# Expert layers: order of the searches and look-ups, look-up table in pairs

## The chip, the cores and the metric

The kernel runs on one core of one Trainium2 chip. The metric is the device time in microseconds; three runs give a median. One execution more is recorded by the hardware profiler, and all rows below come from it.

## The reference, cut to what matters

Two networks run one after the other over 256 tokens of width 1024: a two-layer block (attention and SwiGLU) and then a second two-layer block, whose feed-forward part is an expert lookup. The change touches only that part, which runs twice, once for each layer of the second block:

```python
def peer_ffn(h, w_q, sub_keys, u_tab, v_tab):
    q = (h @ w_q).reshape(B, S, PEER_HEADS, 2, PEER_DQ // 2)
    scores = jnp.einsum('bshpd,hpkd->bshpk', q, sub_keys)
    s1, i1 = lax.top_k(scores[..., 0, :], 16)
    s2, i2 = lax.top_k(scores[..., 1, :], 16)
    cand_s = (s1[..., :, None] + s2[..., None, :])      # 16 x 16 candidates
    cand_id = (i1[..., :, None] * 128 + i2[..., None, :])
    top_s, top_pos = lax.top_k(cand_s, 16)
    ids = jnp.take_along_axis(cand_id, top_pos, axis=-1)
    gate = jax.nn.softmax(top_s, axis=-1)
    ...
    act = jax.nn.gelu(jnp.einsum('thkd,td->thk', u_tab[idx], hx))
    return jnp.einsum('thk,thkd->td', g * act, v_tab[idx])
```

There are 8 heads and 128 x 128 = 16384 experts, each with a row of 1024 in `u_tab` and in `v_tab`.

## The kernel before

`peer(l)` doesn't gather rows. It multiplies all tokens with all experts, 128 tiles of 128 experts each, and sets to zero what wasn't chosen. `M` holds [128, 128 tiles, 256 tokens]: the GELU of each product times its gate.

- *Scores and first level.* 16 products with `wq` give the queries, `score` multiplies them with the keys, and `first_level` finds the 16 best of 128 for each of 16 half heads and both token halves `a` on VectorE (lines 1629 to 1633; maximum, index, replacement, maximum, index: 32 such searches).
- *Expert tiles.* The loop over `NEXP` = 128 calls `u_tile(i)`: a weight tile `raw` of 128 x 1024 is loaded from `pu` by SP's queue; ScalarE rounds it to `hi` (L258); `lo` = `raw` - `hi` is made on VectorE or GpSimd (L259), as `lo_pat` says, "V" or "P"; TensorE then runs 16 products with `hi` and 8 with `lo` (L320), the `hi` ones first. `raw`, `hi` and `lo` have three buffers each. ScalarE applies GELU (L1771).
- *The side list.* `todo` holds the expert choice and the gates as entries (cost, function), some with "P". After each `u_tile` the loop looks at the first entry: with "P" the next tile's `lo` goes to GpSimd and the budget grows by 2.4, else it goes to VectorE and the budget grows by 1.7. Entries are issued as long as the budget covers the first one's cost.
- *The entries.* `second_level(h, a)`: 16 x 16 sums (L1667) and the same five search steps (L1671 to L1675), 8 heads for each token half. `begin(a)`: subtracts the maximum (L1691), copies the first-level indices to a BF16 table `IB` (L1692) and splits the found positions into row and column (`HS`). `look_up(s, a)`: compares with all 16 numbers (L1701), multiplies with the table (L1702), and adds up in halves (L1704, L1705). `exponents`: one exponential on ScalarE for both halves (L1708). `weights`: sum, reciprocal, product. `turn(a)`: three transposes on TensorE (L1725) and copies. `gates(g)`: 64 entries, for four tokens each, which build one-hot operands on VectorE (L1746, L1750), multiply them on TensorE (L1756), and apply the gate to the tiles of `M` already made on VectorE (L1761) or leave it for tiles to come by ScalarE (L1763).
- *Order.* Each engine works through its queue in order. The queue isn't the source's order: a planner at compile time, with its own estimate of durations, places each instruction when its operands are ready, the source's order deciding among ready ones. What it places early and what isn't ready on the chip holds up all behind it.

After the loop `accumulate_tokens` multiplies `M` with the 128 tiles of `pv` (L1442 to L1444).

Of the kernel before, what the change touches and what calls it, by code (L numbers as in the profile page):

```python
# [13 lines left out]
U32 = mybir.dt.uint32  # L14
AF = mybir.ActivationFunctionType
ALU = mybir.AluOpType
# [155 lines left out]
class Kernel:  # L172
# [1310 lines left out]
    def lru(self, l):  # L1483
        nc, tc, A = self.nc, self.tc, self.A
        with self.stream(3, 3), tc.tile_pool(name="lru", bufs=1) as pool:
# [7 lines left out]
            IG = pool.tile([128, 2, KT, T], F32, name="IG")  # L1493
            HS = pool.tile([128, 2, KT, T], F32, name="HS")
            self.begin_mod(pool, l, 0, [A["lruin"][n] for n in range(8)], Y, norm=False, squares=HS[:, 0])

            late = pool.tile([128, 3], F32, name="late")

            def zero_after(i, x):
                nc.scalar.activation(late[:, i:i + 1], x, AF.Relu, scale=-1.0)  # L1500
# [20 lines left out]
            for b in range(4):  # L1521
# [4 lines left out]
                for d in range(2):  # L1526
                    hi, lo = self.wsplit(A["lrug"][b, d], (2, 2, 2, 128))
                    for gt in range(2):
# [7 lines left out]
                        for n in range(2):  # L1536
# [6 lines left out]
                            if gt == 0:  # L1543
                                nc.scalar.activation(HS[:, d, k], R[:, d, k], AF.Tanh, scale=w[:, 4, c:c + 1])
                    k2 = slice(2 * b, 2 * b + 2)
# [22 lines left out]
            for i in range(4):  # L1568
                for d in range(2):
                    x = HS[:, d, 2 * i:2 * i + 2]  # L1570
                    nc.scalar.activation(x, x, AF.Sqrt, bias=late[:, 1:2])
            zero_after(2, HS[:, 1, KT - 1, 0:1])

            def recurrence(i):
                ks = slice(2 * i, 2 * i + 2)
                for d in range(2):
                    nc.vector.tensor_tensor(IG[:, d, ks], IG[:, d, ks], HS[:, d, ks], op=ALU.mult)
                    rv = (lambda x: x[:, ::-1]) if d else (lambda x: x)
# [23 lines left out]
    def peer(self, l):  # L1602
        nc, tc, A = self.nc, self.tc, self.A
        with ExitStack() as st:
# [6 lines left out]
            SI = [tail[:, 512 + a * 256:768 + a * 256].rearrange("p (h j) -> p h j", j=16) for a in range(2)]  # L1611
# [4 lines left out]
            IDX = scratch[:, 3072:3840].rearrange("p (i t) -> p i t", t=T)  # L1616
            HB = scratch[:, 3840:4096].rearrange("p (s h j) -> p s h j", h=8, j=16)
# [33 lines left out]
            for hp in range(16):  # L1651
                p, b = self.product(A["wq"][l, hp], gpool,
                                    (IDX[:, 0, 2 * hp:2 * hp + 2], EQ[:, 1024 + hp % 4 * 256:1280 + hp % 4 * 256]))
# [4 lines left out]
            score(15)  # L1658

            todo = deque()  # L1660
            TOP = [IDX[:, 0, a * 128:a * 128 + 128].rearrange("p (h j) -> p h j", j=16) for a in range(2)]
            POS = [IDX[:, 1, a * 128:a * 128 + 128].rearrange("p (h j) -> p h j", j=16) for a in range(2)]

            def second_level(h, a):
                ca, cb = CA[h % 2], CB[h % 2]
                s1, s2 = SV[a][:, 2 * h], SV[a][:, 2 * h + 1]
                nc.vector.tensor_tensor(ca.rearrange("p (a b) -> p a b", b=16),  # L1667
                                        s1[:, :, None].to_broadcast([128, 16, 16]),
                                        s2[:, None, :].to_broadcast([128, 16, 16]), op=ALU.add)
                t, ix = TOP[a][:, h], POS[a][:, h].bitcast(U32)  # L1670
                nc.vector.max(t[:, 0:8], ca)  # L1671
                nc.vector.max_index(ix[:, 0:8], t[:, 0:8], ca)
                nc.vector.match_replace(cb, t[:, 0:8], ca, -3e38)
                nc.vector.max(t[:, 8:16], cb)
                nc.vector.max_index(ix[:, 8:16], t[:, 8:16], cb)  # L1675
# [2 lines left out]

            spare = scratch[:, 4096:4608].bitcast(BF16)
            KK = spare[:, 0:256].rearrange("p (k j) -> p k j", j=16)  # L1680
            HS = spare[:, 256:512].rearrange("p (s h j) -> p s h j", h=8, j=16)
            IB = spare[:, 512:768].rearrange("p (h s j) -> p s h j", s=2, j=16)
            both = EQ.bitcast(BF16)
            EB = both[:, 0:2048].rearrange("p (h k j) -> p h k j", k=16, j=16)
            ws = IDX[:, 2].rearrange("p (h j) -> p h j", j=16)

            def begin(a):
                if a == 0:
                    nc.vector.tensor_copy(KK, self.iota[:, 0:16, None].to_broadcast([128, 16, 16]))
                pos = POS[a].bitcast(U32)  # L1690
                nc.vector.tensor_tensor(ws[:, 8 * a:8 * a + 8], TOP[a], TOP[a][:, :, 0:1].to_broadcast([128, 8, 16]),  # L1691
                                        op=ALU.subtract)  # L1692
                nc.vector.tensor_copy(IB, SI[a].bitcast(U32).rearrange("p (h s) j -> p s h j", s=2))
                nc.vector.tensor_scalar(HB[:, 0].bitcast(U32), pos, 4, None, op0=ALU.logical_shift_right)
                nc.vector.tensor_scalar(HB[:, 1].bitcast(U32), pos, 15, None, op0=ALU.bitwise_and)
                nc.vector.tensor_copy(HS, HB.bitcast(U32))

            def look_up(s, a):
                tt = nc.vector.tensor_tensor
                all_ = [128, 8, 16, 16]  # L1700
                tt(EB, HS[:, s, :, None, :].to_broadcast(all_), KK[:, None].to_broadcast(all_), op=ALU.is_equal)  # L1701
                tt(EB, EB, IB[:, s, :, :, None].to_broadcast(all_), op=ALU.mult)  # L1702
                for n in (8, 4, 2):
                    tt(EB[:, :, :n], EB[:, :, :n], EB[:, :, n:2 * n], op=ALU.add)  # L1704
                tt((TOP[a], POS[a])[s], EB[:, :, 0], EB[:, :, 1], op=ALU.add)  # L1705

            def exponents():
                nc.scalar.activation(ws, ws, AF.Exp)  # L1708

            def weights():  # L1710
                st_ = gpool.tile([128, 2, 16], F32, name="gst", tag="gst", bufs=1)
# [10 lines left out]
            def turn(a):  # L1722
                p = self.ps("ax")
                for i in range(3):
                    nc.tensor.transpose(p[:, i * 128:i * 128 + 128], IDX[:, i, a * 128:a * 128 + 128], self.ident)  # L1725
                ts = slice(a * 128, a * 128 + 128)
                nc.scalar.activation(CT[:, :, ts], p[:, :256].rearrange("p (a b) -> p a b", b=128), AF.Copy)
                w, rest = p[:, 256:384], scratch[:, :128]
                for i in range(3):
                    nc.vector.tensor_copy(W3[:, i, ts], w)  # L1730
                    if i < 2:
                        nc.vector.tensor_tensor(rest, w, W3[:, i, ts], op=ALU.subtract)
                        w = rest
# [44 lines left out]
            def v_operands(i):  # L1778
# [4 lines left out]
                if i == 8:  # L1783
# [5 lines left out]

            second = [[(2.4, lambda h=h, a=a: second_level(h, a), "P") for h in range(8)] for a in range(2)]  # L1790
            turns = [(1.0, lambda a=a: turn(a)) for a in range(2)]
            gate = [(2.2, lambda g=g: gates(g)) for g in range(ng)]
            decode = [[(1.6, lambda a=a: begin(a))] + [(4.8, lambda s=s, a=a: look_up(s, a)) for s in range(2)]
                      for a in range(2)]

            decode[1][2:2] = [(0.0, exponents)]
            todo.extend(second[0] + decode[0] + second[1] + decode[1] + [(0.9, weights), (2.4, lambda: None)])
            todo.extend(turns + gate)
            budget = 0.0
            for i in range(NEXP):  # L1800
# [138 lines left out]
```

## Time and profile before

| | us |
|---|---|
| median of 3 runs | 3066.19 (3064.2 to 3067.69) |
| the profiled execution | 3063.65 |
| its span, first to last instruction | 3061.8 |
| TensorE products busy | 2979.8 (97%) |
| VectorE busy | 2377.9 (78%) |
| ScalarE busy | 1694.7 (55%) |
| GpSimd busy | 176.1 (6%) |
| mean granted TensorE clock | 0.989 |

The profile calls TensorE PE, its weight loads PEld, VectorE DVE, ScalarE ACT and GpSimd POOL. A share over the whole span is a mean over some twenty stages with different limits. What the change is worth has to be read from the stretches in which its instructions lie: about 1287 to 1430 us for layer 0 and 2234 to 2380 us for layer 1 up to the first gates. An idle time in brackets behind a row is that of its engine just before the row, with what ended it.

### The profile page before, as it was taken

To read this page: it belongs to the slowest core of one execution; us is meant where nothing else is said; L and a number is where in the kernel's file an instruction comes from. 1 tells how busy PE (TensorE), PEld (TensorE's weight loads), DVE (VectorE), ACT (ScalarE), POOL (GpSimd) and SP (SyncE) were. 2 spreads that over 40 slices of the span, in tenths; PEclk is the share of its full clock that TensorE was granted. 3 is DMA by queue.
4 is the path that set the end of the run, shared out by engine and by line. 5 is a ranking of instruction groups with operands and counts; after the bars stand their busy time and mean duration, and the time that the engine had idled before them with its cause. 6 is when DMAs were issued, how large, how long until landed. Compare 5 with 4: busy or idle time off the path is not lost.

```text
span 3061.8 us, 53557 instructions
## 1 busy us (share of the span) xinstructions
PE 2979.8 (97%) x20336; PEld 2705.8 (88%) x20336; DVE 2377.9 (78%) x4869; ACT 1694.7 (55%) x3072; POOL 176.1 (6%) x90
## 2 busy tenths in 40 slices
PE   9999999999999999999999999999898999999998
PEld 8888889888688889999999988888898999988887
DVE  8877997986689698798889655557999888855555
ACT  7556755665565467544554555556744555455554
POOL 0000000000100000351000000000062000000000
PEclk9999999999999999999999999999999999999999
DMA  8853785984059533444444555555444444455554
GB/s 308 277 170 97 241 297 180 313 277 156 24 173 311 164 123 125 143 155 158 155 156 153 172 193 193 193 195 183 149 142 156 161 154 157 158 187 193 194 194 140
DMA packets 155346, 556.57 MB, mean 182 GB/s; under 512 B 17360, under 2 KB 19152, under 8 KB 154832
## 3 DMA queue, kind: packets, MB, share of 16 engines
q1 hardware_dynamic: 154800, 552.62, 54.0%
q8 instruction: 160, 2.62, 0.3%
q14 instruction: 98, 0.80, 0.1%
q10 hardware_dynamic: 288, 0.52, 0.1%
HBM read 552.02 MB, written 1.05 MB: 181 GB/s over the span
## 4 chain that ended last, share of the span: by engine, by line
PE 84%; DVE 11%; ACT 3%; issue 1%; DMA 1%; SPq 0%; DVEq 0%; ACTq 0%
PE ps_mm L320 25%; PE ps_mm L339 14%; PE ps_ax L1442 8%; PE ps_ax L1443 8%; PE ps_ax L1444 8%; PE ps_mm L342 7%; PE ps_mm L1756 3%; PE ps_ax L320 2%; PE ps_mm L671 1%; DVE lo L259 1%; PE ps_ax L1279 1%; DVE M L1667 1%; DMA raw<-in_gu_dram 1%; ACT hi L258 1%; DVE M L1631 1%
## 5 line engine op out<-in xcount | busy, mean ns | idle before, releaser
L258 ACT ACTIVATE hi<-raw 128x1024 fp32r<-128x1024 f32 (+1 forms) x952 | 996.1, 1049 | 963.5 <-PE ps_ax L1443 332.6
L259 DVE TENSOR_TENSOR lo<-raw,hi 128x1024 fp32r<-128x1024 f32 (+1 forms) x898 | 1082.8, 1208 | 532.9 <-ACT hi L258 521.7
L320 PE MATMUL ps_mm<-XX,hi 128*128 128x256 f32 (+1 forms) x5664 | 782.9, 288 | 32.4 <-ACT hi L258 20.5
L320 PEld LDWEIGHTS ps_mm<-XX,hi 128*128 128x128 f32 x5664 | 717.4, 191 | 40.3 <-ACT hi L258 21.1
L320 PE MATMUL ps_mm<-XX,lo 128*128 128x256 f32 (+1 forms) x2832 | 408.1, 284 | 9.5 <-DVE lo L259 9.5
L1444 PE MATMUL ps_ax<-lo,ah 128*128 128x512 f32 x1024 | 398.4, 389 | 0.0
L1443 PE MATMUL ps_ax<-hi,al 128*128 128x512 f32 x1024 | 398.4, 389 | 0.0
L1442 PE MATMUL ps_ax<-hi,ah 128*128 128x512 f32 x1024 | 398.3, 389 | 0.0
L320 PEld LDWEIGHTS ps_mm<-XX,lo 128*128 128x128 f32 x2832 | 368.9, 191 | 11.7 <-DVE lo L259 11.5
L339 PE MATMUL ps_mm<-XX,hi 128*128 128x512 f32 x1216 | 308.7, 395 | 2.8 <-ACT sg L501 2.2
L339 PEld LDWEIGHTS ps_mm<-XX,hi 128*128 128x128 f32 x1216 | 218.2, 189 | 44.1 <-ACT sg L501 3.2
L1444 PEld LDWEIGHTS ps_ax<-lo,ah 128*128 128x128 f32 x1024 | 192.3, 188 | 40.1
L1442 PEld LDWEIGHTS ps_ax<-hi,ah 128*128 128x128 f32 x1024 | 192.3, 188 | 39.8
L1443 PEld LDWEIGHTS ps_ax<-hi,al 128*128 128x128 f32 x1024 | 192.3, 188 | 39.6
L259 POOL TENSOR_TENSOR lo<-raw,hi 128x1024 fp32r<-128x1024 f32 x58 | 147.7, 2555 | 1367.7 <-ACT hi L258 1328.7
L342 PEld LDWEIGHTS ps_mm<-XX,lo 128*128 128x128 f32 x1216 | 163.6, 188 | 17.4 <-DVE lo L259 5.0
L339 PE MATMUL ps_mm<-AHL,hi 128*128 128x512 f32 x704 | 177.7, 392 | 0.0
L342 PE MATMUL ps_mm<-XX,lo 128*128 128x256 f32 x1216 | 169.1, 281 | 1.8 <-DVE lo L259 1.7
L1763 ACT ACTIVATE M<-ps_mm 128x376 f32<-128x376 f32 (+42 forms) x128 | 44.7, 349 | 182.8 <-DVE M L1761 182.8
L339 PEld LDWEIGHTS ps_mm<-AHL,hi 128*128 128x128 f32 x704 | 125.6, 188 | 21.9
L1750 DVE TENSOR_TENSOR oh<-first,W 128x768 bf16<-128x768 bf16 x256 | 130.8, 550 | 0.0
L990 DVE SCALAR_TENSOR_TENSOR raw<-raw,one,cb 128x1024 f32<-128x1024 f32 x96 | 122.9, 1281 | 1.5
(455 smaller groups left out, 3754.0 us busy)
## 6 DMA issues: line engine op xcount, KB each, us to landing
raw<-in_pu_dram SPq DMA_DIRECT2D x256, 512.0 KB, 3.2
raw<-in_pv_dram SPq DMA_DIRECT2D x256, 512.0 KB, 3.2
raw<-in_gu_dram SPq DMA_DIRECT2D x175, 512.0 KB, 4.8
raw<-in_ada_dram SPq DMA_DIRECT2D x96, 512.0 KB, 4.5
raw<-in_down_dram SPq DMA_DIRECT2D x64, 512.0 KB, 4.6
raw<-in_hgin_dram SPq DMA_DIRECT2D x32, 512.0 KB, 3.3
raw<-in_wq_dram SPq DMA_DIRECT2D x32, 512.0 KB, 3.2
raw<-in_down_dram SPq DMA_DIRECT2D x32, 384.0 KB, 3.9
```

The lines of the kernel that those rows point to most:

```text
L258: self.nc.scalar.activation(hi, src, AF.Copy)
L259: (eng or self.lo_engine()).tensor_tensor(lo, src, hi, op=ALU.subtract)
L320: mm(out, w[a][:, k], xin[b][:, k0 + k], start=k0 == 0 and at == 0, stop=k0 + n == kt and at == 3 * n - 1)
L339: mm(p.rearrange("p (a t) -> p a t", a=2), hi[:, k], xin[:, k0 + k], start=k0 + k == 0, stop=False, skip_group_check=True)
L342: mm(p[:, :T], lo[:, k], xin[:, k0 + k, 0], start=False, stop=k0 + k == kt - 1, skip_group_check=True)
L990: nc.vector.scalar_tensor_tensor(w, w, tick, cb, op0=ALU.mult, op1=ALU.mult, accum_out=self.MOD[:, l, j:j + 1])
L1442: m(o, xh[:, ts], hi[:, cs], start=t == 0, stop=False)
L1443: m(o, xl[:, ts], hi[:, cs], start=False, stop=False)
L1444: m(o, xh[:, ts], lo[:, cs], start=False, stop=t == n - 1)
L1750: nc.vector.tensor_tensor(oh[:, q, 1:], first[:, q, None].to_broadcast([128, 3, 128, 2]), W3[:, :, None, t0 + 2 * q:t0 + 2 * q + 2].to_bro ...
L1756: nc.tensor.matmul(p[:, at:at + 128], oh[:, q, 0, :, t], oh[:, q, 1 + n, :, t], start=n == 0, stop=n == 2)
L1763: nc.scalar.activation(M[:, n:, ts], pv[:, n:], AF.Copy)
```

## The change

The side list is put in another order: a first entry of cost 12.0 with "P" that does nothing, then all 16 `second_level`, then both `begin`, then the four `look_up`, with `exponents` ahead of the last. Before it was 8 `second_level`, one `begin`, two `look_up`, and the same for the other token half. The costs of `begin` and `look_up` change with it. `pin` is `keep_in_program_order`: it ties an instruction behind the one issued just before it on the same engine in the source; that is an order in the queue and no wait for its end. It is put on each step of `look_up`, on the exponential and on the transposes of `turn`. The table `IB` now holds each number twice, side by side, so that L1702 reads it in pairs; `HS` and `IB` exist once for each token half.

```diff
--- before.py
+++ after.py
@@ -1658,6 +1658,8 @@
             score(15)
 
             todo = deque()
+
+            pin = tc.keep_in_program_order
             TOP = [IDX[:, 0, a * 128:a * 128 + 128].rearrange("p (h j) -> p h j", j=16) for a in range(2)]
             POS = [IDX[:, 1, a * 128:a * 128 + 128].rearrange("p (h j) -> p h j", j=16) for a in range(2)]
 
@@ -1678,10 +1680,13 @@
 
             spare = scratch[:, 4096:4608].bitcast(BF16)
             KK = spare[:, 0:256].rearrange("p (k j) -> p k j", j=16)
-            HS = spare[:, 256:512].rearrange("p (s h j) -> p s h j", h=8, j=16)
-            IB = spare[:, 512:768].rearrange("p (h s j) -> p s h j", s=2, j=16)
+            HS = [spare[:, a * 256 + 256:a * 256 + 512].rearrange("p (s h j) -> p s h j", h=8, j=16) for a in range(2)]
             both = EQ.bitcast(BF16)
             EB = both[:, 0:2048].rearrange("p (h k j) -> p h k j", k=16, j=16)
+
+            EB2 = both[:, 0:2048].rearrange("p (m q two) -> p m q two", q=8, two=2)
+            IB = [both[:, a * 512 + 2048:a * 512 + 2560].rearrange("p (s m two) -> p s m two", s=2, two=2)
+                  for a in range(2)]
             ws = IDX[:, 2].rearrange("p (h j) -> p h j", j=16)
 
             def begin(a):
@@ -1690,22 +1695,25 @@
                 pos = POS[a].bitcast(U32)
                 nc.vector.tensor_tensor(ws[:, 8 * a:8 * a + 8], TOP[a], TOP[a][:, :, 0:1].to_broadcast([128, 8, 16]),
                                         op=ALU.subtract)
-                nc.vector.tensor_copy(IB, SI[a].bitcast(U32).rearrange("p (h s) j -> p s h j", s=2))
+                numbers = SI[a].bitcast(U32).rearrange("p (h s) j -> p s h j", s=2)
+                for s in range(2):
+                    nc.vector.tensor_copy(IB[a][:, s].rearrange("p (h j) two -> p h j two", j=16),
+                                          numbers[:, s, :, :, None].to_broadcast([128, 8, 16, 2]))
                 nc.vector.tensor_scalar(HB[:, 0].bitcast(U32), pos, 4, None, op0=ALU.logical_shift_right)
                 nc.vector.tensor_scalar(HB[:, 1].bitcast(U32), pos, 15, None, op0=ALU.bitwise_and)
-                nc.vector.tensor_copy(HS, HB.bitcast(U32))
+                nc.vector.tensor_copy(HS[a], HB.bitcast(U32))
 
             def look_up(s, a):
-                tt = nc.vector.tensor_tensor
+                tt = lambda *x, **kw: pin(nc.vector.tensor_tensor(*x, **kw))
                 all_ = [128, 8, 16, 16]
-                tt(EB, HS[:, s, :, None, :].to_broadcast(all_), KK[:, None].to_broadcast(all_), op=ALU.is_equal)
-                tt(EB, EB, IB[:, s, :, :, None].to_broadcast(all_), op=ALU.mult)
+                tt(EB, HS[a][:, s, :, None, :].to_broadcast(all_), KK[:, None].to_broadcast(all_), op=ALU.is_equal)
+                tt(EB2, EB2, IB[a][:, s, :, None, :].to_broadcast([128, 128, 8, 2]), op=ALU.mult)
                 for n in (8, 4, 2):
                     tt(EB[:, :, :n], EB[:, :, :n], EB[:, :, n:2 * n], op=ALU.add)
                 tt((TOP[a], POS[a])[s], EB[:, :, 0], EB[:, :, 1], op=ALU.add)
 
             def exponents():
-                nc.scalar.activation(ws, ws, AF.Exp)
+                pin(nc.scalar.activation(ws, ws, AF.Exp))
 
             def weights():
                 st_ = gpool.tile([128, 2, 16], F32, name="gst", tag="gst", bufs=1)
@@ -1722,7 +1730,7 @@
             def turn(a):
                 p = self.ps("ax")
                 for i in range(3):
-                    nc.tensor.transpose(p[:, i * 128:i * 128 + 128], IDX[:, i, a * 128:a * 128 + 128], self.ident)
+                    pin(nc.tensor.transpose(p[:, i * 128:i * 128 + 128], IDX[:, i, a * 128:a * 128 + 128], self.ident))
                 ts = slice(a * 128, a * 128 + 128)
                 nc.scalar.activation(CT[:, :, ts], p[:, :256].rearrange("p (a b) -> p a b", b=128), AF.Copy)
                 w, rest = p[:, 256:384], scratch[:, :128]
@@ -1790,11 +1798,13 @@
             second = [[(2.4, lambda h=h, a=a: second_level(h, a), "P") for h in range(8)] for a in range(2)]
             turns = [(1.0, lambda a=a: turn(a)) for a in range(2)]
             gate = [(2.2, lambda g=g: gates(g)) for g in range(ng)]
-            decode = [[(1.6, lambda a=a: begin(a))] + [(4.8, lambda s=s, a=a: look_up(s, a)) for s in range(2)]
-                      for a in range(2)]
-
-            decode[1][2:2] = [(0.0, exponents)]
-            todo.extend(second[0] + decode[0] + second[1] + decode[1] + [(0.9, weights), (2.4, lambda: None)])
+
+            todo.append((12.0, lambda: None, "P"))
+            todo.extend(second[0] + second[1] + [(2.0, lambda a=a: begin(a)) for a in range(2)])
+
+            todo.extend([(4.1, lambda s=s, a=a: look_up(s, a)) for a in range(2) for s in range(2)])
+            todo.insert(len(todo) - 1, (0.0, exponents))
+            todo.extend([(0.9, weights), (2.4, lambda: None)])
             todo.extend(turns + gate)
             budget = 0.0
             for i in range(NEXP):
```

## Rows read from the trace of the kernel before

**Rows 1.** Busy us by stretches: start:end, length, engines, granted clock, DMA share, GB/s
```profile
1375.00:1400.00 25.00, 19.25 (x139) 19.05 (x139) 24.79 (x59) 9.86 (x14) 12.48 (x5) 0.86 0.33 110
...
1650.00:1675.00 25.00, 25.00 (x249) 24.66 (x249) 22.91 (x44) 12.53 (x29) 0.00 (x0) 1.00 0.50 161
```

**Rows 2.** TensorE in order of time, layer 0: start, us, instruction, [idle before]
```profile
1320.12 2.06 PE L320 MATMUL ps_mm<-XX,hi 128*128 128x256 f32 x16
...
1342.90 2.06 PE L320 MATMUL ps_mm<-XX,hi 128*128 128x256 f32 x16
1348.81 2.08 PE L320 MATMUL ps_mm<-XX,lo 128*128 128x256 f32 x8 [3.85 <-DVE lo L259]
...
1389.76 3.79 PE L320 MATMUL ps_mm<-XX,hi 128*128 128x256 f32 x16 [5.75 <-ACT hi L258]
...
1424.94 0.49 PE L1725 MATMUL ps_ax<-c_ident,M 128*128 128x128 f32 x3
```

**Rows 3.** TensorE in order of time, layer 1
```profile
2270.53 2.06 PE L320 MATMUL ps_mm<-XX,hi 128*128 128x256 f32 x16
...
2340.56 3.78 PE L320 MATMUL ps_mm<-XX,hi 128*128 128x256 f32 x16 [8.78 <-ACT hi L258]
...
2375.76 0.49 PE L1725 MATMUL ps_ax<-c_ident,M 128*128 128x128 f32 x3
```

**Rows 4.** VectorE in order of time: last first-level search, first `lo`; last search, layer 1
```profile
1337.46 0.28 DVE L1633 FIND_INDEX8 M<-M 128x8 uint32<-128x128 f32 x1
...
1347.54 1.21 DVE L259 TENSOR_TENSOR lo<-raw,hi 128x1024 fp32r<-128x1024 f32 x1
...
2285.04 0.28 DVE L1633 FIND_INDEX8 M<-M 128x8 uint32<-128x128 f32 x1
```

**Rows 5.** ScalarE in order of time: the exponential, layer 0 and layer 1
```profile
1375.96 1.28 ACT L1708 ACT_TABLE_LOAD   x1
1386.65 0.42 ACT L1708 ACTIVATE M<-M 128x256 f32<-128x256 f32 x1 [9.41 <-DVE M L1691]
...
2337.45 0.42 ACT L1708 ACTIVATE M<-M 128x256 f32<-128x256 f32 x1 [10.79 <-DVE M L1691]
```

**Rows 6.** The additions L1667 from 1286, from 1336.4 (ns min/median/max), and single ones
```profile
L1667 DVE TENSOR_TENSOR M<-M x9: 400/440/1806, 1295.3 to 1345.8; 128x256 f32<-128x256 f32 x9
L1667 DVE TENSOR_TENSOR M<-M x5: 400/412/440, 1337.0 to 1345.8; 128x256 f32<-128x256 f32 x5
...
1369.69 1.84 DVE L1667 TENSOR_TENSOR M<-M 128x256 f32<-128x256 f32 x1
1373.29 0.80 DVE L1667 TENSOR_TENSOR M<-M 128x256 f32<-128x256 f32 x1
...
1380.95 0.41 DVE L1667 TENSOR_TENSOR M<-M 128x256 f32<-128x256 f32 x1
1383.12 0.40 DVE L1667 TENSOR_TENSOR M<-M 128x256 f32<-128x256 f32 x1
```

**Rows 7.** GpSimd by lines from 1319 to 1340 and from 1364 to 1380: busy, mean ns
```profile
L259 POOL TENSOR_TENSOR lo<-raw,hi 128x1024 fp32r<-128x1024 f32 x6 | 14.4, 2394 | 4.1 <-ACT hi L258 3.6 <-DMA raw<-in_pu_dram 0.5
L259 POOL TENSOR_TENSOR lo<-raw,hi 128x1024 fp32r<-128x1024 f32 x5 | 13.8, 2787 | 27.9 <-ACT hi L258 27.9
```

**Rows 8.** VectorE in order of time, one look-up; then L1750 by lines
```profile
1399.21 1.22 DVE L1701 TENSOR_TENSOR M<-M 128x2048 bf16<-128x2048 bf16 x1
1400.47 2.29 DVE L1702 TENSOR_TENSOR M<-M 128x2048 bf16<-128x2048 bf16 x1
1402.68 1.22 DVE L259 TENSOR_TENSOR lo<-raw,hi 128x1024 fp32r<-128x1024 f32 x1
1403.82 1.47 DVE L1704 TENSOR_TENSOR M<-M 128x1024 bf16<-128x1024 bf16 x3
1405.32 0.29 DVE L1705 TENSOR_TENSOR M<-M 128x128 f32<-128x128 bf16 x1
...
L1750 DVE TENSOR_TENSOR oh<-first,W 128x768 bf16<-128x768 bf16 x256 | 130.8, 550 | 0.0
```

## The prediction

> **What bounds the kernel now.** I read the busy time by stretches first, then TensorE's order of time in the two stretches that stood out, then VectorE's and ScalarE's there, because those two are named as what TensorE waits for. TensorE is the bound: in an ordinary stretch of an expert layer it is busy for all 25 us and VectorE for 22.91 [rows 1]. In the stretch from 1375 us it is busy for 19.25 only, the granted clock is 0.86, and VectorE is busy for 24.79 [rows 1]. So the two `peer` layers have a place where VectorE, else hidden, is late.
>
> TensorE's rows give the loss. Undisturbed, eight tiles of `u_tile` take 1342.90 - 1320.12 = 22.78 us, 2.8475 each [rows 2]. From tile 1 (1320.12) to the first transpose of `turn` (1424.94) are 104.82 us. Replaying the list `todo` with its budget puts `turn(0)` behind tile 31, so 31 tiles lie between: 31 x 2.8475 = 88.27 us of work and 16.55 us lost. Layer 1 has the same list: 2375.76 - 2270.53 = 105.23, 16.96 lost [rows 3]. **Together 33.5 us** are what the change can win. The loss has two causes in the rows of each layer:
>
> - VectorE is late for the first tile whose `lo` it makes (tile 9; tiles 0 to 8 are on GpSimd). That `lo` starts at 1347.54, behind first-level searches that end only at 1337.46, second-level searches and `begin(0)` [rows 4]; TensorE waits 3.85 us [rows 2].
> - ScalarE stands still. `exponents` sits in its queue ahead of the `hi` of later tiles and waits 9.41 us for the subtraction of `begin(1)` (L1691), in layer 1 10.79 us [rows 5]. VectorE reaches that subtraction late, because the second half of the searches lies before it. TensorE waits 5.75 and 8.78 us for `hi` [rows 2, 3].
>
> After a wait the products run at the lower clock level for a while: the 16 products behind the second wait take 3.79 us instead of 2.06 [rows 2]. In layer 0 the two waits are 9.60 of 16.55 us; the other 6.95 are such slow products and small waits, so a wait costs itself and about 3.5 us.
>
> **The change part by part.**
>
> *Searches first, five idle tiles.* By the replay tiles 0 to 21 now have their `lo` on GpSimd (before: 0 to 8 and 16 to 23), all 16 second-level searches are issued over tiles 5 to 20, and tile 22 is the first whose `lo` VectorE makes. At TensorE's pace tile 22 starts at 1320.12 + 21 x 2.8475 = 1379.92; its `lo` products come 2.06 us later and the `lo` takes 1.21 [rows 4], so VectorE has to begin it by 1380.8. What has to be done before that: the first level ends at 1337.7 as now, with four second-level searches done by then (of nine additions L1667 in that view five start after 1336.4 [rows 6]); twelve remain. The price of one is the distance between two L1667: 2.17 us with GpSimd idle (1380.95 to 1383.12), 3.60 at worst while GpSimd works (1369.69 to 1373.29), and 2.56 (2.17 and the 0.39 by which an addition of 0.80 is longer) for the next one [rows 6]. GpSimd works during all of this stretch, one `lo` for each tile, so I take one search for each tile, 2.85 us: 34.2. The two `begin` are some seven small instructions each, none larger than the addition of 0.41 us: at most 5.8 us, I take 2.4. Sum 1337.7 + 34.2 + 2.4 = 1374.3, 6.5 us early. Bounds: 1363.7 and 1386.7 (5.9 late). Layer 1: first level to 2285.3 [rows 4], the deadline is 2270.53 + 59.80 + 0.85 = 2331.2, done at 2321.9, between 2311 and 2334.3 (3.1 late). So the first wait goes in both layers at the middle price.
>
> GpSimd must keep pace for 22 tiles on end: its `lo` takes 2.394 us alone and 2.787 us beside second-level searches [rows 7], both below 2.8475. It keeps up by 0.06 us a tile, so this part costs nothing; if it were 0.1 over, 22 tiles would lose 2 us, less than the two tiles that it runs ahead. The loads of `raw` on SP's queue wait for the same `lo` and go no later than now.
>
> *`exponents` pinned.* It now stands behind the GELU of tile 30 and its operand comes from `begin(1)`, issued at tile 23: seven tiles, 20 us. It waits for nothing then. Queued behind it on ScalarE are `hi` and GELU of later tiles, and TensorE needs those. It still costs the 0.42 us and two table loads of 1.28 [rows 5], 3.0 us, under a `hi` that is made up to two tiles (5.7 us) ahead with three buffers. Hidden, unless VectorE hands out `lo` at the last moment, when `raw` and `hi` come later too. Bounds 0 and 3.0 us a layer; nearest is a `hi` two tiles ahead, but in the look-up stage VectorE is tight (below), so I take 1.5 a layer, 3 in all.
>
> *Look-ups pinned, table in pairs.* A look-up now is 1.26 + 2.21 + 1.50 + 0.29 = 5.26 us by the starts of its steps [rows 8]. The multiplication (L1702) reads a table whose last dimension is a broadcast and takes 2.29 us; the comparison before it, same 2048 elements, takes 1.22. In pairs it has the shape that `gates` uses in L1750: 768 elements in 0.55 us, 1.4 elements/ns against 0.9. Bounds 1.22 and 2.29; I take 1.22, the same element count with steps of one. That gives 4.2 us. Stage from tile 22 to 33: 12 tiles are 34.2 us of TensorE; VectorE has 12 `lo` of 1.14 (start to start) = 13.7, four look-ups 16.8, `begin` 2.4, `weights` about 1.0: 33.9. It is just in balance, and without the faster multiplication it would be 4.3 over, still less than the 6.5 us by which it begins early. A pinned look-up can't slip ahead of the `lo` of the tile before it, and the order is no wait. So this part wins nothing by itself; it keeps the next wait from forming.
>
> *Transposes pinned, gates later.* `turn(0)` moves from tile 31 to 35, three tiles behind the last look-up and two behind `weights`: TensorE waits there only if VectorE is more than 5.7 us behind. The 64 gates start at tile 37 (33 before) and end at tile 118 of 127: no tail. Each then multiplies about 4 tiles x 4 tokens = 16 elements more on VectorE instead of ScalarE, 0.02 us in a stage with 2.09 us in 25 free [rows 1]. The extra copies of `begin` and the second `HS` and `IB` are counted above. No DMA is added or moved.
>
> **The sum.** 33.5 - 3.0 = 30.5 us won. The profiled execution took 3063.65 us (span 3061.8): 3033.2. The median of the runs shown lies 2.54 higher, 3066.19: **3035.7 us**. With nothing of the 3.0 it is 3032.7; with 3.0 a layer 3035.7 + 3 = 3038.7.
>
> **The rivals.**
>
> 1. *The wait moves to tile 22.* VectorE and GpSimd slow each other: L1667 takes 0.40 us with GpSimd idle and 0.80 to 1.84 beside it [rows 6]. If a search costs more than (1380.8 - 2.4 - 1337.7) / 12 = 3.39 us, VectorE is late again. At 3.60: 5.9 + 3.5 in layer 0, 3.1 + 3.5 in layer 1, 16 us back: 3051.7. For: one distance of 3.60. Against: the 2.56 for the next one. Chance 0.15.
> 2. *Every search waits out a whole GpSimd instruction.* Then one costs 2.17 + 2.39 = 4.56, twelve 54.7; VectorE is 14 us late in layer 0 and 11 in layer 1, with 3.5 each 32 us back: about 3068, no change. Against: 1.84 is the longest in rows 6, and the waits get shorter as the two fall into step. Chance 0.05. The Trainium skill, SBUF — State Buffer, section "SBUF: two separate sides", speaks for this one: the port pair that VectorE and GpSimd share is an exclusive lock, held for a whole instruction, and the other blocks. By that rule the longer stretch on GpSimd works against the change; the trace agrees with a block (0.40 against 1.84) but not with a full one each time.
> 3. *Only the pin on `exponents` does what it says.* The searches aren't pinned, and the planner could leave other work ahead of tile 22's `lo`. Then 5.75 + 3.5 and 8.78 + 3.5 are won, 21.5: 3044.7. Chance 0.08.
> 4. *Slower: the gate stage turns to VectorE's pace.* Its room is 2.09 us in 25 [rows 1], 0.24 a tile. If the later gates raise VectorE's work so far that each of the 128 gates delays TensorE by 0.35 us, 45 us are lost: 3080. It decides from 30.5 / 128 = 0.24 us a gate. Against: 0.02 us is what I find. Chance 0.04.
>
> **How the numbers follow.** Forecast 0.68 (3031 to 3040), rivals 0.15, 0.05, 0.08, 0.04. The range 3030 to 3052 holds the forecast and rivals 1 and 3; the low end is the whole 33.5 with the spread of the runs. Within 0.2%, 6 us, is about what a measurement of this kernel can't tell from no change: rival 2. Faster 0.91, same 0.05, slower 0.04.
>
> **What would show it.** Right: no wait for `hi` of 5 us or more on TensorE between the first tile and `turn` in either layer, granted clock 1.00 there; `exponents` waiting under 1 us; L1702's successor near 1.2 us; tile 22's `lo` begun before TensorE needs it; 35 tiles from tile 1 to `turn` in about 100 to 102 us. Wrong: a wait on `lo` at tile 22 (rivals 1, 2), a new wait for `hi` behind `exponents`, gaps among the gates (rival 4), or a time above 3052.

## The result, and the profile after

| | before | after |
|---|---|---|
| median (lowest to highest), 4 runs each, us | 3065.76 (3064.20 to 3067.69) | 3030.20 (3027.61 to 3033.29) |
| profiled execution; its span, us | 3063.65; 3061.8 | 3033.29; 3031.4 |
| mean granted TensorE clock | 0.989 | 0.993 |
| TensorE, VectorE, ScalarE, GpSimd busy, us | 2979.8, 2377.9, 1694.7, 176.1 | 2971.8, 2356.7, 1693.0, 194.2 |

Ratio 0.9888 (95% interval 0.9876 to 0.9899): 35.6 us faster by the medians. The forecast was 3035.7, range 3030 to 3052. The median lies 0.2 us above the low end of that range.

First the stretches, as in [rows 1]: the start and end, length, busy us (and instructions) of TensorE, its weight loads, VectorE, ScalarE and GpSimd, then the granted clock, DMA share and GB/s. Kernel after:

```profile
1350.00:1375.00 25.00, 25.00 (x214) 25.00 (x213) 25.00 (x82) 11.36 (x19) 21.17 (x9) 1.00 0.57 186
1375.00:1400.00 25.00, 25.00 (x213) 25.00 (x212) 20.41 (x31) 11.74 (x18) 2.95 (x2) 1.00 0.61 194
```

The stretch from 1375 us had TensorE busy for 19.25 us at clock 0.86; now it is busy for all 25, at 1.00. One stretch earlier VectorE is busy without a gap and GpSimd for 21.17 us: the searches and the `lo` of those tiles side by side.

TensorE in order of time, after (start, us, instruction), against [rows 2] and [rows 3]:

```profile
1324.22 2.06 PE L320 MATMUL ps_mm<-XX,hi 128*128 128x256 f32 x16
...
1384.00 2.06 PE L320 MATMUL ps_mm<-XX,hi 128*128 128x256 f32 x16
...
1423.86 0.49 PE L1733 MATMUL ps_ax<-c_ident,M 128*128 128x128 f32 x3
...
2257.14 2.06 PE L320 MATMUL ps_mm<-XX,hi 128*128 128x256 f32 x16
...
2316.91 2.06 PE L320 MATMUL ps_mm<-XX,hi 128*128 128x256 f32 x16
...
2356.77 0.49 PE L1733 MATMUL ps_ax<-c_ident,M 128*128 128x128 f32 x3
```

The first and last row of each layer are tile 1 and the first transpose of `turn`, now with 35 tiles between them: 99.64 us in layer 0 and 99.63 in layer 1. 35 x 2.8475 is 99.66. Not a tenth of a microsecond is lost in either layer, and no row between them has a wait. So **all 33.5 us of [rows 2, 3] are won**, where 30.5 were forecast. The other 2 us of the 35.6 are no more than the scatter: the four runs of one kernel lie 3.5 and 5.7 us apart.

In the profiled pair the spans differ by 30.4 us only, since the two executions had drifted apart before the change acts: tile 1 of layer 0 starts at 1324.22 and not at 1320.12. The instructions of VectorE and ScalarE up to the first second-level search of that layer come in the same order in both kernels. A second profiled execution of after (span 3030.1) has its first `turn` at 1422.54, 1.3 us sooner than the first one. TensorE's products too come in the same order up to that point; the profiled execution of after is already 1.2 us behind at 70 us and 4.2 at 950. I take the 4.1 us for scatter between executions; its cause was not looked for.

VectorE in order of time, after. L1669 is the addition that [rows 6] have as L1667; L1696 and L1700 are the subtraction and the number casts of `begin`:

```profile
1342.09 2.33 DVE L1669 TENSOR_TENSOR M<-M 128x256 f32<-128x256 f32 x1
...
1346.97 0.41 DVE L1669 TENSOR_TENSOR M<-M 128x256 f32<-128x256 f32 x1
...
1349.14 0.98 DVE L1669 TENSOR_TENSOR M<-M 128x256 f32<-128x256 f32 x1
...
1363.28 1.08 DVE L1669 TENSOR_TENSOR M<-M 128x256 f32<-128x256 f32 x1
...
1366.12 1.07 DVE L1669 TENSOR_TENSOR M<-M 128x256 f32<-128x256 f32 x1
...
1368.96 1.08 DVE L1669 TENSOR_TENSOR M<-M 128x256 f32<-128x256 f32 x1
...
1374.65 0.95 DVE L1696 TENSOR_TENSOR M<-M 128x128 f32<-128x128 f32 x1
...
1376.47 2.08 DVE L1700 CAST M<-M 128x256 bf16<-128x256 uint32 x1
...
1380.39 2.38 DVE L259 TENSOR_TENSOR lo<-raw,hi 128x1024 fp32r<-128x1024 f32 x2 [0.17 <-PE ps_mm L320]
...
2304.72 1.57 DVE L1696 TENSOR_TENSOR M<-M 128x128 f32<-128x128 f32 x1
...
2306.55 2.15 DVE L1700 CAST M<-M 128x256 bf16<-128x256 uint32 x1
...
2309.03 2.33 DVE L1700 CAST M<-M 128x256 bf16<-128x256 uint32 x1
...
2312.95 1.22 DVE L259 TENSOR_TENSOR lo<-raw,hi 128x1024 fp32r<-128x1024 f32 x1
```

From 1349 us on the additions come every 2.84 us, one for each tile of TensorE. GpSimd at that time, in order:

```profile
1361.67 2.41 POOL L259 TENSOR_TENSOR lo<-raw,hi 128x1024 fp32r<-128x1024 f32 x1 [0.43 <-ACT hi L258]
1364.52 2.40 POOL L259 TENSOR_TENSOR lo<-raw,hi 128x1024 fp32r<-128x1024 f32 x1 [0.44 <-ACT hi L258]
```

The first of these two ends at 1364.08 and the addition begun at 1363.28 at 1364.36; the second ends at 1366.92 and the addition begun at 1366.12 at 1367.19. So each addition ends 0.3 us behind a GpSimd instruction.

Tile 22 starts at 1384.00 in the rows of TensorE, so its `lo` must be begun by 1384.00 + 2.06 - 1.22 = 1384.84; it is begun at 1380.39, **4.5 us early**. In layer 1 it is 2312.95 against 2317.75: 4.8 early.

The exponential on ScalarE, after, against [rows 5]:

```profile
1410.21 1.28 ACT L1716 ACT_TABLE_LOAD   x1
1411.50 0.42 ACT L1716 ACTIVATE M<-M 128x256 f32<-128x256 f32 x1
1411.83 1.04 ACT L258 ACTIVATE hi<-raw 128x1024 fp32r<-128x1024 f32 x1
```

It starts right behind its table load, where it had waited 9.41 us, and the next `hi` right behind it. And GpSimd by lines from 1324.2 to 1424 us, after (busy, mean ns | idle before, releasers), against [rows 7]:

```profile
L259 POOL TENSOR_TENSOR lo<-raw,hi 128x1024 fp32r<-128x1024 f32 x19 | 45.7, 2404 | 9.9 <-ACT hi L258 9.4 <-DMA raw<-in_pu_dram 0.5
```

### The profile page after: what moved, and what is told of

It is laid out like the page before. It is cut to its first block, busy times and chain, and to the rows that moved or that the text cites. A ratio compares the mean times of both kernels' runs of the same rounds, so it can differ in the third digit from the quotient of the medians.

```text
span 3031.4 us, 53540 instructions
## 1 busy us (share of the span) xinstructions
PE 2971.8 (98%) x20336; PEld 2697.5 (89%) x20336; DVE 2356.7 (78%) x4855; ACT 1693.0 (56%) x3070; POOL 194.2 (6%) x100
## 4 chain that ended last, share of the span: by engine, by line
PE 92%; DVE 3%; ACT 3%; DMA 1%; issue 1%; SPq 0%; DVEq 0%; ACTq 0%
PE ps_mm L320 33%; PE ps_mm L339 14%; PE ps_ax L1444 8%; PE ps_ax L1442 8%; PE ps_ax L1443 8%; PE ps_mm L342 7%; PE ps_mm L1764 3%; PE ps_ax L320 2%; PE ps_mm L671 1%; PE ps_ax L1279 1%; DMA raw<-in_gu_dram 1%; DVE lo L259 1%; PE ps_ax L961 1%; PE ps_ax L561 1%; PE ps_ax L1407 1%
## 5 line engine op out<-in xcount | busy, mean ns | idle before, releaser
L259 DVE TENSOR_TENSOR lo<-raw,hi 128x1024 fp32r<-128x1024 f32 (+2 forms) x888 | 1070.5, 1208 | 518.7 <-ACT hi L258 513.0
L259 POOL TENSOR_TENSOR lo<-raw,hi 128x1024 fp32r<-128x1024 f32 x68 | 165.8, 2440 | 1310.3 <-ACT hi L258 1298.4
L1771 ACT ACTIVATE M<-ps_mm 128x360 f32<-128x360 f32 (+42 forms) x128 | 43.0, 336 | 185.5 <-DVE M L1769 185.5
L339 PEld LDWEIGHTS ps_mm<-AHL,hi 128*128 128x128 f32 x704 | 125.7, 188 | 21.9
```

The lines of the kernel that those rows point to most:

```text
L259: (eng or self.lo_engine()).tensor_tensor(lo, src, hi, op=ALU.subtract)
L339: mm(p.rearrange("p (a t) -> p a t", a=2), hi[:, k], xin[:, k0 + k], start=k0 + k == 0, stop=False, skip_group_check=True)
L1771: nc.scalar.activation(M[:, n:, ts], pv[:, n:], AF.Copy)
```

## The experiments

The theory was that the change consists of parts that need each other: the order takes VectorE's wait away, the pins keep the order, the idle tiles make it early enough. The rival was that one of them, the pin on the exponential above all, does most by itself. Each kernel below is before with a part of the change added, or after with a part taken out, and was timed in turns with the kernel before, in two sets. Each time is a median and is set against the median of before in its own set, 3064.04 or 3065.47.

### The pin on the exponential alone

Before, with

```diff
-                nc.scalar.activation(ws, ws, AF.Exp)
+                pin(nc.scalar.activation(ws, ws, AF.Exp))
```

> The kernel before with the pin on the exponential alone. Theory: in the old order VectorE's own queue is the second limit. With the exponential moved from behind GELU 17 to behind GELU 26, nine look-up steps (about 8.7 us) stand ahead of the first lo that VectorE makes after the second half of the searches, so TensorE waits for lo there, about 3 us in layer 0 and 5 in layer 1 with 3.5 us of slow products each: some 7 us won in all, 3059 us. Rival 3 of the prediction: the waits for hi simply go, 21.5 us won, 3045 us.

Measured 3058.43 against 3064.04, ratio 0.9984 (0.9974 to 0.9993): 5.6 us won. TensorE in order of time, with what it waited for in brackets:

```profile
1349.38 2.08 PE L320 MATMUL ps_mm<-XX,lo 128*128 128x256 f32 x8 [3.85 <-DVE lo L259]
...
1399.95 2.08 PE L320 MATMUL ps_mm<-XX,lo 128*128 128x256 f32 x8 [4.98 <-DVE lo L259]
...
2347.80 2.08 PE L320 MATMUL ps_mm<-XX,lo 128*128 128x256 f32 x8 [7.76 <-DVE lo L259]
```

No wait for `hi` is left: the exponential stood behind 18 GELUs of layer 0 in ScalarE's order, and stands behind 27 now. But 10 us after the place of the old wait there is one of nearly its length, for a `lo` of VectorE. VectorE, in order of time, ahead of the 4.98 us:

```profile
1389.05 1.23 DVE L1702 TENSOR_TENSOR M<-M 128x2048 bf16<-128x2048 bf16 x1
...
1398.67 1.22 DVE L259 TENSOR_TENSOR lo<-raw,hi 128x1024 fp32r<-128x1024 f32 x1
```

Between these two rows it is busy with look-up steps, nine with the first, as expected, and the second is the `lo` that TensorE waits for. VectorE was late for both, for `begin(1)` and for the next `lo`; while the exponential stood in front, only the first was to be seen. Rival 3 of the prediction, which gave this pin 21.5 us, falls.

### All pins, in the old order

Before, with the pins on the exponential, the look-ups (`tt = lambda *x, **kw: pin(nc.vector.tensor_tensor(*x, **kw))`) and the transposes.

> The kernel before with all pins, in the old order and without idle tiles and pairs. Theory: the second wait goes, because the exponential stands behind GELU 26 and the look-ups behind their lo; the first wait (3.85 and 2.92 us for lo, with the slow products behind) stays, since the first-level searches still end at 1337 us and tile 9 needs VectorE at 1344 us: 21.5 us won, 3045 us. Rival: the pins do all of it, 3032 us.

Measured 3050.68, ratio 0.9960 (0.9945 to 0.9974): 13.4 us won, not 21.5. TensorE:

```profile
1347.96 2.08 PE L320 MATMUL ps_mm<-XX,lo 128*128 128x256 f32 x8 [3.85 <-DVE lo L259]
...
1396.85 1.25 PE L320 MATMUL ps_mm<-XX,lo 128*128 128x256 f32 x8 [3.45 <-DVE lo L259]
...
2290.24 1.22 PE L320 MATMUL ps_mm<-XX,lo 128*128 128x256 f32 x8 [2.92 <-DVE lo L259]
...
2339.13 1.42 PE L320 MATMUL ps_mm<-XX,lo 128*128 128x256 f32 x8 [3.79 <-DVE lo L259]
```

The first wait of each layer is untouched, as expected: it comes from the order of searches. The second has shrunk and not gone, which I had not expected. VectorE begins the `lo` of that tile right behind the last search and `begin(1)`:

```profile
1395.58 3.49 DVE L259 TENSOR_TENSOR lo<-raw,hi 128x1024 fp32r<-128x1024 f32 x3
```

In the old order the second half of the searches comes only behind two look-ups and the `lo` of seven tiles, so it ends too late for the tile at which `lo` goes back to VectorE, and no pin moves it. This is what the new order is for.

### The new order without any pin

After, with all three pins taken off.

> The changed kernel without any pin. Theory: the new order alone does harm, because the planner puts the exponential behind GELU 11 while the subtraction that it needs now stands behind all 16 searches: ScalarE waits some 24 us, TensorE some 20 us and 3.5 us of slow products in each layer, and the look-ups stand ahead of the first lo: 3075 to 3085 us, slower than before. Rival: the order is what counts and the pins are a detail, 3030 to 3036 us.

Measured 3074.45, ratio 1.0032 (1.0021 to 1.0044): **slower than before**. TensorE:

```profile
1372.53 3.78 PE L320 MATMUL ps_mm<-XX,hi 128*128 128x256 f32 x16 [12.04 <-ACT hi L258]
...
1403.68 2.08 PE L320 MATMUL ps_mm<-XX,lo 128*128 128x256 f32 x8 [6.38 <-DVE lo L259]
...
2327.12 3.79 PE L320 MATMUL ps_mm<-XX,hi 128*128 128x256 f32 x16 [9.87 <-ACT hi L258]
...
2358.28 2.08 PE L320 MATMUL ps_mm<-XX,lo 128*128 128x256 f32 x8 [6.85 <-DVE lo L259]
```

Unpinned, the exponential now stands behind 12 GELUs and not behind 18 as in before, and its table load starts 32.0 us after tile 1 of layer 0 instead of 55.8. Its operand comes sooner too, but only by 17.6 us, so it waits 15.69 us on ScalarE instead of 9.41. The two next runs part the two pins.

### After without the pin on the exponential

> The changed kernel with the exponential not pinned. Theory: it goes behind GELU 11 and waits there for the subtraction behind the 16 searches, some 24 us on ScalarE; TensorE waits some 20 us for hi and has 3.5 us of slow products, in each layer: 3072 to 3080 us. Rival: the searches come early enough now and the pin on the exponential is not needed, 3030 to 3036 us.

Measured 3057.41, ratio 0.9972 (0.9962 to 0.9981): 27.7 us above after in the same set of runs (3029.74). The table load before the exponential, and the exponential, on ScalarE:

```profile
1355.26 1.28 ACT L1716 ACT_TABLE_LOAD   x1
1372.23 0.42 ACT L1716 ACTIVATE M<-M 128x256 f32<-128x256 f32 x1 [15.69 <-DVE M L1696]
```

TensorE:

```profile
1375.34 3.78 PE L320 MATMUL ps_mm<-XX,hi 128*128 128x256 f32 x16 [12.03 <-ACT hi L258]
...
2319.35 3.79 PE L320 MATMUL ps_mm<-XX,hi 128*128 128x256 f32 x16 [9.87 <-ACT hi L258]
```

The place and the kind are those expected, the size is not: 15.7 us on ScalarE instead of about 24. GpSimd and VectorE say why. GpSimd, then VectorE:

```profile
1375.36 7.04 POOL L259 TENSOR_TENSOR lo<-raw,hi 128x1024 fp32r<-128x1024 f32 x3 [17.92 <-ACT hi L258]
```

```profile
1350.94 1.09 DVE L1669 TENSOR_TENSOR M<-M 128x256 f32<-128x256 f32 x1
...
1353.80 1.09 DVE L1669 TENSOR_TENSOR M<-M 128x256 f32<-128x256 f32 x1
...
1359.48 0.41 DVE L1669 TENSOR_TENSOR M<-M 128x256 f32<-128x256 f32 x1
...
1361.65 0.41 DVE L1669 TENSOR_TENSOR M<-M 128x256 f32<-128x256 f32 x1
```

With no `hi`, GpSimd stands still for 17.92 us, and from then on an addition takes 0.41 us instead of 1.09 and a search 2.17 instead of 2.86. So VectorE reaches the subtraction sooner than I had worked out: the one of `begin(1)` ends 48.9 us after the start of tile 1, in after 54.8. That is 5.9 of the 8.3 us between 24 and 15.7; where the rest comes from was not looked for. The same rows measure what GpSimd costs a search: 0.69 us, nearly all of it (0.68) in the addition L1669.

### After without the pin on the look-ups

> The changed kernel with the look-ups not pinned. Theory: the planner puts all 24 look-up steps ahead of tile 22's lo; at 4.2 us for six of them that lo comes 17 us later, 12.7 us after TensorE needs it, with 3.5 us of slow products, in each layer: 32 us more, 3062 us (3054 to 3068). Rival: buffers and the lead of VectorE cover it, 3030 to 3036 us.

Measured 3058.87, ratio 0.9981 (0.9972 to 0.9991): 29.1 us above after, so 6.6 us are left of its gain. TensorE, then VectorE:

```profile
1399.36 2.08 PE L320 MATMUL ps_mm<-XX,lo 128*128 128x256 f32 x8 [12.39 <-DVE lo L259]
...
2344.87 2.08 PE L320 MATMUL ps_mm<-XX,lo 128*128 128x256 f32 x8 [11.76 <-DVE lo L259]
```

```profile
1382.06 1.22 DVE L1710 TENSOR_TENSOR M<-M 128x2048 bf16<-128x2048 bf16 x1
...
1398.09 3.49 DVE L259 TENSOR_TENSOR lo<-raw,hi 128x1024 fp32r<-128x1024 f32 x3
```

All 24 steps of the four look-ups lie in one block ahead of the `lo` of tile 22, some 17 us that TensorE doesn't need yet. In after, four `lo` come before the first step.

### After without the idle tiles

After, with

```diff
-            todo.append((12.0, lambda: None, "P"))
```

> The changed kernel without the first entry of cost 12.0, so that tile 17 is the first whose lo VectorE makes. Theory: the idle tiles give VectorE time; it was 4.5 and 4.9 us early at tile 22, the deadline comes 14.24 us earlier, and GpSimd stops earlier too, so the last searches cost 2.17 instead of 2.85 us: 5.3 us late in layer 0 and 2.6 in layer 1, with 3.5 us of slow products each, 15 us more than the changed kernel, 3045 us (3040 to 3052). Rival: the searches float ahead anyway and the idle tiles give nothing, 3030 us.

Measured 3040.84 against 3064.04, ratio 0.9929 (0.9912 to 0.9946): 23.2 us won, 12.5 less than after in the other set. TensorE:

```profile
1371.70 2.08 PE L320 MATMUL ps_mm<-XX,lo 128*128 128x256 f32 x8 [3.15 <-DVE lo L259]
...
2307.64 2.08 PE L320 MATMUL ps_mm<-XX,lo 128*128 128x256 f32 x8 [2.89 <-DVE lo L259]
```

One wait in each layer, at tile 17, which is now the first whose `lo` VectorE makes. From tile 1 to the first `turn`, 30 tiles here, TensorE takes 90.34 and 91.28 us, 4.9 and 5.9 more than 30 x 2.8475; in after nothing is lost there. So the idle entry does no work and still holds some 11 us: it leaves five more tiles to GpSimd.

### After with the look-up table in single copies

After, with

```diff
-                tt(EB2, EB2, IB[a][:, s, :, None, :].to_broadcast([128, 128, 8, 2]), op=ALU.mult)
+                tt(EB, EB, IB[a][:, s, :, :, None].to_broadcast(all_), op=ALU.mult)
```

and a table of 256 elements, written by one cast.

> The changed kernel with the old look-up table, one copy of each number. Theory: the multiplication goes back to 2.29 us, 4.3 us more on VectorE in each layer, which its lead and the waits for hi between its lo cover: as the changed kernel within 2 us, 3028 to 3034 us. Rival: the look-up stage is VectorE's, each microsecond counts, 4.3 us and 3.5 us of slow products in each layer, 3040 to 3046 us.

Measured 3031.54, ratio 0.9892 (0.9876 to 0.9909); after in the same set has 0.9884 (0.9867 to 0.9900). No difference can be seen. VectorE:

```profile
1403.38 2.28 DVE L1705 TENSOR_TENSOR M<-M 128x2048 bf16<-128x2048 bf16 x1
```

The multiplication takes 2.28 us instead of the 1.22 of the paired table (L1710 above). The price was forecast right, and TensorE has no wait in either kernel: the 4.3 us of each layer lie in room that nothing else needs.

### After, once more

> The changed kernel once more, beside the three below: 3028 to 3034 us by either theory. It gives the time that the three are read against.

Measured 3029.74 against 3065.47, ratio 0.9884 (0.9867 to 0.9900), and again no wait of TensorE in the two stretches.

### The transposes

No run takes out the pin on the transposes alone. But TensorE's products come in the same order in after as in the new order without any pin, and in the old order the same with all pins as with the exponential's alone. So this pin moves nothing on TensorE; what it is worth by itself was not timed.

**Together.** Won against before, in us:

| kernel | won | waits of TensorE left in the two stretches, us |
|---|---|---|
| exponential's pin alone | 5.6 | 20.1, most for `lo` |
| all pins, old order | 13.4 | 15.7, `lo` |
| new order, no pin | -10.4 | 35.4, `hi` and `lo` |
| after without the exponential's pin | 8.1 | 21.9, `hi` |
| after without the look-ups' pin | 6.6 | 24.2, `lo` |
| after without the idle tiles | 23.2 | 6.0, `lo` |
| after without pairs | 33.9 | none |
| after | 35.7 | none |

The whole gain needs the order, two pins and the idle tiles. Without the exponential's pin or the look-ups' pin, three quarters and more of the gain is gone.

## Why the prediction was right, step by step

**The loss and its two causes: right.** 33.5 us were to be won, and both stretches now run at 2.847 us a tile. The two causes are shown separately: the wait for the first `lo` stays when only pins are set (3.85 us), and the wait for the exponential comes back, longer, when only its pin is taken out.

**The searches' price: right.** Taken were 2.85 us for each of the twelve, one a tile. The rows give 2.84. One addition, begun at 1342.09, takes 2.33 us, nearly a whole GpSimd instruction (2404 ns), as rival 2 wanted for all of them; from the second behind it on the two engines are nearly in step, and soon each addition loses 0.67 us. Rival 1 (3.60 each) and rival 2 (4.56) fall. That GpSimd keeps pace held too: 2404 ns a `lo`, nearer to the 2394 than to the 2787 of [rows 7], with searches beside it all the time.

**The two `begin`: mis-sized.** Taken were 2.4 us, at most 5.8. From the first subtraction to the first `lo` are 1380.39 - 1374.65 = 5.74 us in layer 0 and 2312.95 - 2304.72 = 8.23 in layer 1, each with some 0.75 us of the last search in it. In the kernel without idle tiles, where GpSimd stands still then, the same stretch of layer 0 takes 3.24 us (1367.18 to 1370.42). So the instructions were counted right, and what was missing is 2.5 and 5.0 us of waiting for GpSimd: the cast L1700 takes 2.08, 2.15 and 2.33 us beside it and 0.27 without, and the subtraction L1696 0.95 and 1.57 instead of 0.27. The bound took the addition of 0.41 us for the longest that an instruction here can be, which is an addition with GpSimd idle. The margin at tile 22 was 4.5 and 4.8 us instead of 6.5 and 9.3; at some 2 us for a cast, three more of them would have used it up (an estimate). The Trainium skill, SBUF — State Buffer, section "Who interferes with whom", says that a cast in a two-port mode contends with GpSimd: whichever issues first has the shared pair of ports for its whole instruction, and the other is blocked. The casts of 2.08 to 2.33 us against 2404 ns agree with this; that they ran in such a mode no run here shows.

**The exponential's reserve: mis-sized.** 3.0 us were held back for table loads and the queue behind it. Its wait is 0 and no `hi` is late, so the cost is 0, which was the lower bound. Without the reserve the sum gives 3032.7, within 2.5 us of the median of 3030.20.

**The look-ups.** The paired multiplication takes 1.22 us, as taken. "This part wins nothing by itself" holds for the pairs. For the pin it was too weak: order that is no wait sounded like order that is cheap, and the pin holds 29.1 us. Without it the forecast would have been missed altogether. What I had not asked is where the instructions would stand if they were not pinned.

**Rival 3: wrong in its size.** It took the waits for `hi` as won by the pin (21.5 us). The run gave 5.6, because the same late VectorE stood behind both waits.

**3.5 us of slow products for each wait: too high.** From tile 1 to the first `turn` of both layers, against 2.8475 us a tile, 28.5 us are lost without the look-ups' pin, 26.7 without the exponential's and 10.8 without idle tiles. Less the waits of the table, for each of the two waits: (28.5 - 24.2) / 2 = 2.2, (26.7 - 21.9) / 2 = 2.4, (10.8 - 6.0) / 2 = 2.4. In before all waits of the two stretches add up to 24.0 of the 33.5 us, which leaves 2.4 for each of the four long ones; the 3.5 had small waits in it. It entered the rivals only.

**The gates: right.** The stage of gates by stretches (columns as above), the same 265 us from the first `turn` of layer 0, before and then after:

```profile
1425.00:1690.00 265.00, 265.00 (x2571) 262.18 (x2570) 232.29 (x461) 136.26 (x291) 0.00 (x0) 1.00 0.47 156
```

```profile
1424.00:1689.00 265.00, 265.00 (x2572) 262.20 (x2570) 233.27 (x462) 135.32 (x291) 0.00 (x0) 1.00 0.46 156
```

VectorE has 0.98 us more over the 60 gates of these 265 us, 0.016 each where 0.02 was taken, and ScalarE 0.94 less; TensorE is busy all the time in both. Rival 4 falls.

**The number: in part luck.** 3030.20 lies below the 3031 to 3040 that had a chance of 0.68, and only 0.2 us inside the range; the later median of after, 3029.74, lies outside it. What the sum had too much of is the reserve of 3.0 us. The `begin`, dearer than their bound in layer 1 (8.23 - 0.75 = 7.48 against 5.8), cost nothing only because the searches left a margin large enough for them.

## What to carry to other kernels

A wait that ends on a certain engine can hide a later lateness of that engine: before an edit is credited with a wait, ask what the late engine owes next. Here the pin alone won 5.6 us of 21.5 for that reason. Where a planner places instructions, an order in the source is worth nothing until it is known where the planner puts them; the same order was 35.7 us faster with pins and 10.4 slower without. And a step in the source that does no work can be the one that sets which engine gets which tile.

## What the runs showed of the hardware

- Two engines that disturb each other fell into step. One early addition beside GpSimd took 2.33 us, the later ones 1.08, and with GpSimd idle 0.41. The longest value of a short stretch (1.84 in [rows 6]) was no price for a long one; one search for each GpSimd instruction was, since each addition ended 0.3 us behind one.
- A small instruction paid as long a wait as a larger one: a cast of 256 elements in each partition, 0.27 us alone, took up to 2.33 beside GpSimd, twice the 1.22 of a whole `lo`.
- The length of a wait did not decide by itself what it cost in clock. In after without the exponential's pin, the 3.78 us of products behind the wait of 12.03 us ran at a granted clock of 0.50 (1.2 of 2.4 GHz). In after without idle tiles, the products behind a wait of 2.89 us took 2.08 us, also at 0.50. With all pins in the old order, those behind a wait of 2.92 us took 1.22 at 1.00. I had priced every wait alike, and what tells the last two apart stays open.
